# Top-256 search of a sparse attention: the largest score tiles counted by sums of signs on ScalarE instead of by comparisons on VectorE, with one more pass for equal scores

## The chip, the cores and the metric

The kernel runs on one core of a Trainium2 chip. The metric is the device time of one execution in microseconds (us). The profile shows the engines of that core: PE is TensorE's matrix multiply (PEld its weight loads), DVE is VectorE, ACT is ScalarE, POOL is GpSimd, SP is SyncE. In this program SP issues the transfers.

## The reference, cut to what matters

The program is a decoder trunk of two layers over 1024 tokens of width 1024. Each layer has an input projection, three groups of attention heads, an output projection, a gated FFN and a gated embedding. One of the groups is sparse: every query keeps only the 256 earlier positions with the highest index score, and its softmax runs over those.

```python
ilog = jnp.einsum('bqhd,bkd->bqhk', sl(idx_q), idx_k) * IDX_DIM ** -0.5
isc = jnp.einsum('bqhk,bqh->bqk', jax.nn.relu(ilog), sl(idx_w)).astype(jnp.float32)
isc = jnp.where(causal[None], isc, -jnp.inf)
_, sel = lax.top_k(isc, topk)          # topk = 256; of equal scores the earlier positions
valid = sel <= qpos[None, :, None]
...
a = jnp.where(valid[:, None], a, -jnp.inf)
pa = jax.nn.softmax(a, axis=-1).astype(vg.dtype)
```

## The kernel before

The tokens are handled in two halves of 512. For each layer and half there is dense work (`in_projection`, `layer_rest`: `gemm` with three matmuls for each 128x128 block of weights, lines 266 to 268) and attention work (`attention`). `weave` (line 64) interleaves the two by weights, so that the attention of one part runs between the dense matmuls of another. PE's order is written out by the program itself; for the other engines a scheduler decides the order from priorities. Every engine works through its own order strictly from front to back.

`attention(L, half)` begins with `indexer`, which fills the score tile `isc` (lines 1046 to 1050). It holds one block of columns for each query tile of 128 tokens that can have more than 256 candidates: in half 0 tiles of 384 and 512 columns, in half 1 of 640, 768, 896 and 1024. Then a list of steps is worked off, five stick-breaking heads, six latent heads, five sparse heads. A step of a head has its parts in `scores` (line 788, into PSUM), `piece` (line 828, PE transposes the probabilities into PSUM tile T), `post_piece` (lines 835 and 836: ACT rounds T to the high part of `PT`, DVE subtracts to get the low part) and `pv` (line 845, PE multiplies `PT` with the values into O).

The search, `topk` (lines 1070 to 1114), is a generator that runs in the background of the stick and latent heads. It finds the 256th largest score of each row bit by bit: 31 times (line 1094) `count` compares each tile with that row's candidate and adds up the hits (line 1082, one DVE instruction for each tile, followed in the trace by a read of its accumulator), line 1096 turns the counts into a bit, line 1097 sets the next candidate. A first count decides the sign of the threshold, a last one counts the scores above it, and lines 1107 to 1113 turn `isc` into a mask. All of this is on DVE. The loop that works off the steps gives the search a credit with each step (`TOPK_W`, lines 57, 1156 and 1172) and draws pieces of it while credit is left (line 1176); before the first sparse head it draws the rest (line 1167):

```python
background = topk()
tk = TOPK_W[half] / max(first_sparse - 1, 1)
...
credit += tk * (TOPK_RATE[0] if step < SB_H * nb else TOPK_RATE[1])
...
    while credit > 0:
        credit -= next(background, 1e9)
```

Other lines that the prediction names: `rstd` (lines 344 to 352), twelve small DVE instructions in a chain that give the norm of 512 tokens, with `replicate` (line 360) on PE behind them; line 187, ACT's rounding of a weight tile; `norm` of a pair of heads (line 938), which copies sums into the small tile `wide` for PE to transpose; line 888, DVE's scan of a stick head; line 874, ACT's exponential with its sum.

Of the kernel before, what the change touches and what calls it, by code (L numbers as in the profile page):

```python
# [8 lines left out]
F32 = mybir.dt.float32  # L9
R = mybir.dt.float32r  # L10
BF = mybir.dt.bfloat16
I32 = mybir.dt.int32
AF = mybir.ActivationFunctionType
ALU = mybir.AluOpType
AX = mybir.AxisListType

T = 1024
# [4 lines left out]
HALF = 512  # L22
# [4 lines left out]
TOPK = 256  # L27
EPS = 1e-6
NEG = -1e30
# [12 lines left out]
PTS, AS, VS = 2, 2, 2  # L42
# [11 lines left out]
LAG = (3, 3)  # L54
DENSE = {"in": 1188, "full": 2622, "last": 2028}
ATT = (256, 500, 356, 400)
TOPK_W = (51, 157)


def f32(ap):  # L60
# [28 lines left out]
def trunk(ctx: ExitStack, tc, x, p, w_in, attn_norm, mla_q_norm, mla_w_uq, mla_kv_norm, mla_w_ukv,  # L89
# [3 lines left out]
    PE, ACT, DVE, POOL = nc.tensor, nc.scalar, nc.vector, nc.gpsimd  # L93
# [7 lines left out]
    ap = pool("ap", 1)  # L101
    sm = pool("sm", 4)
# [613 lines left out]
    def attention(L, half):  # L716
        k = (L, half)
        nk = HALF * (half + 1)
        tiles = [4 * half + i for i in range(4)]
        itiles = [t for t in tiles if t >= 2]  # L720
        off, o = {}, 0
        for t in itiles:
            off[t] = o
            o += 128 * (t + 1)
        isc = ap.tile([128, 3328], F32, name="isc")

        def have(*keys):
            return all(clock[0] - stored.get(key, 1e9) >= DELAY for key in keys)
# [175 lines left out]
        class Head:  # L904
# [26 lines left out]
            def norm(self):  # L931

                j = self.i // 2
                if self.done and j in rows:
                    self.n = n = 64 if self.i % 2 == 0 else 128
                    self.S = S_tile()[:, 0]
                    wide = sm.tile([128, 4, 2, 64], F32, name="wide", bufs=1)
                    ACT.copy(wide[:, :, :n // 64], rows[j].rearrange("p h t -> p t h")[:, :, :n // 64].unsqueeze(
                        3).to_broadcast([128, 4, n // 64, 64]))
                    for t in range(4):  # L940
                        PE.transpose(self.S[:n, t * 128:(t + 1) * 128],
                                     wide[:, t, :n // 64].rearrange("p h c -> p (h c)"), identF)
# [126 lines left out]
                    yield 0.5 + (t + 1) * 0.5  # L1069
        def topk():  # L1070

            ni = len(itiles)

            def small(name, dt):
                return sm.tile([128, 4], dt, name=name, bufs=1)[:, :ni]
            cnt, xm, cand, inc = small("cnt", F32), small("xm", I32), small("cand", I32), small("inc", I32)
            junk = ap.tile([128, T], mybir.dt.uint8, name="junk")

            def count(c, op):
                for i, t in enumerate(itiles):  # L1080
                    n = 128 * (t + 1)
                    DVE.tensor_scalar(junk[:, :n], isc[:, off[t]:off[t] + n], c[:, i:i + 1], None,  # L1082
                                      op0=op, op1=ALU.add, accum_out=cnt[:, i:i + 1])
                    yield 0.13 + n / 960

            DVE.memset(cand, 0)
            yield from count(cand.bitcast(F32), ALU.is_ge)


            DVE.tensor_scalar(inc, cnt, float(TOPK), None, op0=ALU.is_ge)  # L1090
# [1 line left out]
            DVE.tensor_scalar(xm, inc, -1, None, op0=ALU.bitwise_xor)  # L1092
            DVE.tensor_scalar(cand, xm, 1 << 30, None, op0=ALU.bitwise_xor)
            for b in range(30, -1, -1):
                yield from count(cand.bitcast(F32), ALU.is_ge)
                DVE.tensor_scalar(inc, cnt, float(TOPK), float(1 << b), op0=ALU.is_lt, op1=ALU.mult)
                DVE.scalar_tensor_tensor(cand, inc, (1 << b) >> 1, cand, op0=ALU.bitwise_xor, op1=ALU.bitwise_xor)
                yield 0.2
            thr = cand.bitcast(F32)
            yield from count(thr, ALU.is_gt)  # L1100
            DVE.tensor_scalar(cnt, cnt, -1.0, float(TOPK), op0=ALU.mult, op1=ALU.add)
            for i, t in enumerate(itiles):
                n = 128 * (t + 1)
                s = isc[:, off[t]:off[t] + n]
                c = slice(i, i + 1)
# [3 lines left out]
                                       op0=ALU.mult, op1=ALU.add)  # L1109
# [45 lines left out]
        background = topk()  # L1155
        tk = TOPK_W[half] / max(first_sparse - 1, 1)
        credit = 0.0
# [141 lines left out]
```

## Time and profile before

| | |
|---|---|
| median of 3 runs | 3207.02 us (3206.75 to 3208.24) |
| the profiled execution's own time | 3211.26 us |
| its span, first to last instruction | 3209.1 us |
| PE busy | 3068.6 us (96%) |
| DVE busy | 2099.0 us (65%) |
| ACT busy | 1486.3 us (46%) |
| POOL busy | 1722.9 us (54%) |
| DVE's counts for the search (line 1082 with the reads of its accumulator) | 371.3 + 32.1 us |

Busy times of a whole span are averages over stages with different limits. The stages matter here: the profile cuts the span into 40 slices of 80 us and gives each engine's busy tenths, and the trace can be asked for any stretch. The search runs in four stretches, one for each layer and half, of which the two of half 1 are the long ones.

### The profile page before, as it was taken

To read this page: it belongs to the slowest core of one execution; us is meant where nothing else is said; L and a number is where in the kernel's file an instruction comes from. 1 tells how busy PE (TensorE), PEld (TensorE's weight loads), DVE (VectorE), ACT (ScalarE), POOL (GpSimd) and SP (SyncE) were. 2 spreads that over 40 slices of the span, in tenths; PEclk is the share of its full clock that TensorE was granted. 3 is DMA by queue.
4 is the path that set the end of the run, shared out by engine and by line. 5 is a ranking of instruction groups with operands and counts; after the bars stand their busy time and mean duration, and the time that the engine had idled before them with its cause. 6 is when DMAs were issued, how large, how long until landed. Compare 5 with 4: busy or idle time off the path is not lost. (4 is left out here: it accounts for less than half of the span.)

```text
span 3209.1 us, 43576 instructions
## 1 busy us (share of the span) xinstructions
PE 3068.6 (96%) x15059; PEld 2549.1 (79%) x15059; DVE 2099.0 (65%) x3701; ACT 1486.3 (46%) x2485; POOL 1722.9 (54%) x1980
## 2 busy tenths in 40 slices
PE   8889999999998999999999999889999999999998
PEld 7768888777887888888888788767888877888877
DVE  4878656799997646687744636899997465322234
ACT  4555654445445545444444535544444455322234
POOL 4533356666445433765555744656445445766665
PEclk9999999999999999999999999999999999999999
DMA  7465453323233346433333465422333323333322
GB/s 203 117 194 147 144 172 96 91 89 96 90 97 93 105 116 176 132 103 107 107 104 89 116 162 176 116 72 86 98 97 95 89 70 113 117 99 94 98 92 73
DMA packets 549949, 363.59 MB, mean 113 GB/s; under 512 B 134672, under 2 KB 491744, under 8 KB 549728
## 3 DMA queue, kind: packets, MB, share of 16 engines
q1 hardware_dynamic: 549727, 360.81, 38.7%
q8 instruction: 119, 1.95, 0.3%
q14 instruction: 103, 0.84, 0.1%
HBM read 310.65 MB, written 50.08 MB: 112 GB/s over the span
## 5 line engine op out<-in xcount | busy, mean ns | idle before, releaser
L196 POOL TENSOR_TENSOR wl<-wr,wh 128x256 fp32r<-128x256 f32 x1684 | 1375.4, 848 | 1178.5 <-ACT wh L187 1143.9
L266 PE MATMUL D<-act,wh 128*128 128x512 f32 x3416 | 1363.6, 399 | 31.6 <-DVE h L582 16.5
L267 PE MATMUL D<-act,wh 128*128 128x512 f32 x3416 | 1341.0, 393 | 2.3 <-DVE act L633 2.0
L268 PE MATMUL D<-act,wl 128*128 128x512 f32 x3416 | 1340.0, 392 | 2.4 <-POOL wl L196 2.4
L266 PEld LDWEIGHTS D<-act,wh 128*128 128x128 f32 x3416 | 646.0, 189 | 174.7 <-issue 14.1
L268 PEld LDWEIGHTS D<-act,wl 128*128 128x128 f32 x3416 | 645.3, 189 | 145.9 <-POOL wl L196 4.8
L187 ACT CAST wh<-wr 128x1024 fp32r<-128x1024 f32 (+3 forms) x432 | 443.6, 1027 | 665.6 <-PE D L267 525.5
L267 PEld LDWEIGHTS D<-act,wh 128*128 128x128 f32 x3416 | 646.6, 189 | 126.6 <-DVE act L633 3.1
L1082 DVE TENSOR_SCALAR_CACHE_REDUCE junk<-isc,cand 128x512 uint8<-128x512 f32 (+5 forms) x396 | 371.3, 938 | 5.5
L836 DVE TENSOR_TENSOR PT<-T,PT 128x384 fp32r<-128x384 f32 (+1 forms) x320 | 201.8, 631 | 139.9 <-ACT PT L835 138.9
L835 ACT CAST PT<-T 128x384 fp32r<-128x384 f32 (+1 forms) x320 | 173.6, 542 | 192.4 <-PE T L828 181.4
L845 PEld LDWEIGHTS O<-PT,V 128*128 128x128 f32 x1280 | 196.2, 190 | 72.2 <-DVE PT L836 43.7
L845 PE MATMUL O<-PT,V 128*128 128x256 f32 x1280 | 215.5, 287 | 38.1 <-DVE PT L836 34.3
L891 POOL TENSOR_TENSOR P<-P,A 128x127 f32<-128x127 f32 (+3 forms) x80 | 101.0, 1266 | 198.3 <-DVE A L888 122.1
L788 PE MATMUL S<-kh,qh 128*128 128x384 f32 (+4 forms) x544 | 206.6, 381 | 0.3 <-ACT P L1042 0.3
L788 PE MATMUL S<-kl,qh 128*128 128x384 f32 (+4 forms) x544 | 203.8, 375 | 1.6 <-DVE kl L293 1.6
L828 PE MATMUL T<-identF,P 128*128 128x128 f32 x1152 | 182.2, 277 | 17.5 <-POOL P L891 6.6
L828 PEld LDWEIGHTS T<-identF,P 128*128 128x128 f32 x1152 | 135.4, 142 | 21.9 <-POOL P L891 9.0
L1048 DVE SCALAR_TENSOR_TENSOR isc<-P,iw,isc 128x384 f32<-128x384 f32 (+2 forms) x84 | 97.0, 1157 | 78.4 <-ACT P L1042 78.3
L619 POOL TENSOR_TENSOR tmp<-tmp,rr 128x512 f32<-128x512 f32 x88 | 120.2, 1366 | 32.4 <-DVE tmp L618 27.0
L630 DVE SCALAR_TENSOR_TENSOR tmp<-tmp,D 128x512 f32<-128x512 f32 x88 | 60.1, 683 | 107.6 <-POOL tmp L619 80.3
L853 ACT COPY o<-O 64x256 f32<-64x256 f32 x128 | 47.3, 370 | 175.4 <-PE O L845 174.0
(217 smaller groups left out, 3304.4 us busy)
## 6 DMA issues: line engine op xcount, KB each, us to landing
wr<-in_w_gate_dram SPq DMA_DIRECT2D x88, 512.0 KB, 3.8
wr<-in_w_up_dram SPq DMA_DIRECT2D x88, 512.0 KB, 3.8
wr<-in_w_down_dram SPq DMA_DIRECT2D x80, 512.0 KB, 3.4
wr<-in_w_in_dram SPq DMA_DIRECT2D x44, 512.0 KB, 3.8
wr<-in_w_in_dram SPq DMA_DIRECT2D x76, 256.0 KB, 3.8
wr<-in_w_o_dram SPq DMA_DIRECT2D x32, 512.0 KB, 4.3
wr<-in_w_ple_gate_dram SPq DMA_DIRECT2D x32, 512.0 KB, 3.8
h<-h SPq DMA_DIRECT2D x56, 256.0 KB, 4.4
```

The lines of the kernel that those rows point to most:

```text
L187: ACT.copy(hi, raw)
L196: POOL.tensor_tensor(l[:, ks], a[:, ks], f32(h[:, ks]), op=ALU.subtract)
L266: PE.matmul(ps, a, ah, start=first and i == 0, stop=False)
L267: PE.matmul(ps, a, al, start=False, stop=False)
L268: PE.matmul(ps, b, ah, start=False, stop=last and i == len(ks) - 1)
L619: POOL.tensor_tensor(t, t, ffn.rep, op=ALU.mult)
L788: PE.matmul(o, a, b, start=j == 0, stop=j == len(mms) - 1)
L828: PE.transpose(ps[:, o:o + 128], self.P[q][:, j * 128:(j + 1) * 128], identF)
L835: ACT.copy(pt[:, 0, o:], self.ps[:, o:])
L836: DVE.tensor_sub(pt[:, 1, o:], self.ps[:, o:], f32(pt[:, 0, o:]))
L845: PE.matmul(self.O[:, :256], self.head.V[:, j, :], pt[:, s, o:o + 256], start=j == 0 and s == 0, stop=j == 2 * self.n - 1 and s == 1)
L1082: DVE.tensor_scalar(junk[:, :n], isc[:, off[t]:off[t] + n], c[:, i:i + 1], None, op0=op, op1=ALU.add, accum_out=cnt[:, i:i + 1])
```

## The change

In each half the last tiles (one of 512 columns in half 0; those of 896 and 1024 in half 1, the first padded with -1e30 to 1024) are no longer compared by DVE in the 31 rounds. ACT takes sign(2^24 * (candidate - score)) over the tile and sums it, which is the number of scores below the candidate less the number above it. A small ACT instruction scales the candidates first (`bias`), and one more DVE instruction of each round turns the sums into bits. Since a score equal to the candidate adds 0 to a sum of signs, the rounds can end one step off where scores are equal; after them one more count of all tiles against the next larger number, with nine small DVE instructions, settles that. `wide` no longer has a tile of its own and takes a buffer of the tile name `A` (2 buffers, also used by the stick heads' line 886 and by the search's lines 1106 to 1113). The credits follow the shorter DVE work.

```diff
-TOPK_W = (51, 157)
+TOPK_W = (40, 96)
+SCALE, LEAST = 2.0 ** 24, 2.0 ** -126
...
+        na, wa = ((1, 512), (2, 1024))[half]
         off, o = {}, 0
-        for t in itiles:
+        for i, t in enumerate(itiles):
             off[t] = o
-            o += 128 * (t + 1)
-        isc = ap.tile([128, 3328], F32, name="isc")
+            o += 128 * (t + 1) if i < len(itiles) - na else wa
+        isc = ap.tile([128, 3456], F32, name="isc")
+        for t in itiles[-na:]:
+            if 128 * (t + 1) < wa:
+                POOL.memset(isc[:, off[t] + 128 * (t + 1):off[t] + wa], NEG)
...
-                    wide = sm.tile([128, 4, 2, 64], F32, name="wide", bufs=1)
+                    wide = ap.tile([128, T], F32, name="A", bufs=AS)[:, :HALF].rearrange(
+                        "p (t h c) -> p t h c", t=4, h=2)
...
+            nv = ni - na
...
+            def signs(i):
+                o = off[itiles[nv + i]]
+                ACT.activation(junk2[:, :wa], isc[:, o:o + wa], AF.Sign, scale=-SCALE, bias=bias[:, i:i + 1],
+                               accum_out=sgn[:, i:i + 1])
...
             for b in range(30, -1, -1):
-                yield from count(cand.bitcast(F32), ALU.is_ge)
-                DVE.tensor_scalar(inc, cnt, float(TOPK), float(1 << b), op0=ALU.is_lt, op1=ALU.mult)
+                ACT.activation(bias, c[:, nv:], AF.Copy, scale=SCALE)
+                for i in range(max(nv, na)):
+                    if i < na:
+                        signs(i)
+                    if i < nv:
+                        yield count(i, c, ALU.is_ge)
+                DVE.tensor_scalar(inc[:, :nv], cnt[:, :nv], float(TOPK), float(1 << b), op0=ALU.is_lt, op1=ALU.mult)
+                DVE.tensor_scalar(inc[:, nv:], sgn, float(wa + 1 - 2 * TOPK), float(1 << b), op0=ALU.is_gt, op1=ALU.mult)
                 DVE.scalar_tensor_tensor(cand, inc, (1 << b) >> 1, cand, op0=ALU.bitwise_xor, op1=ALU.bitwise_xor)
-                yield 0.2
-            thr = cand.bitcast(F32)
-            yield from count(thr, ALU.is_gt)
+                yield 0.4
+
+            nxt, ok = small("nxt", F32), small("ok", F32)
+            DVE.tensor_scalar(nxt.bitcast(I32), cand, 0x7fffffff, None, op0=ALU.bitwise_and)
+            DVE.tensor_scalar(ok, nxt, LEAST, None, op0=ALU.is_ge)
+            DVE.tensor_mul(c, c, ok)
+            DVE.tensor_scalar(nxt, nxt, 0.6 * 2.0 ** -23, None, op0=ALU.mult)
+            DVE.tensor_add(nxt, nxt, c)
+            for i in range(ni):
+                yield count(i, nxt, ALU.is_ge)
+            DVE.tensor_scalar(ok, cnt, float(TOPK), None, op0=ALU.is_ge)
+            DVE.tensor_sub(nxt, nxt, c)
+            DVE.tensor_mul(nxt, nxt, ok)
+            DVE.tensor_add(c, c, nxt)
+            thr = c
+            for i in range(ni):
+                yield count(i, thr, ALU.is_gt)
```

PE's order is the same before and after, but for the name of the tile that line 938's sums are transposed from. The orders of DVE and ACT move. In the changed program's listing the lines stand higher: 344 to 352 become 345 to 353, 835 and 836 become 841 and 842, 888 becomes 894, 1082 becomes 1095; 1114 is the small `bias`, 1101 the sum of signs, 1120 and 1121 the two bit instructions.

The first place is DVE in layer 1, half 1, where the first norm that falls into the search computes its `rstd` (the FFN norm of layer 1's half 0). Before, its first twelve instructions from `ms` on are these; the chain goes on to a third `rstd` with four more counts between (640, 768, 896, 1024 columns):

```order
2303 L344 TENSOR_SCALAR ms<-T 128x4
2304 L1082 TENSOR_SCALAR junk,cnt<-isc,cand 128x768
2305 L347 TENSOR_SCALAR rtmp<-ms 128x4
2306 L1082 TENSOR_SCALAR junk,cnt<-isc,cand 128x896
2307 L348 TENSOR_SCALAR rstd<-rtmp 128x4
2308 L1082 TENSOR_SCALAR junk,cnt<-isc,cand 128x1024
2309 L350 TENSOR_TENSOR rtmp<-rstd 128x4
2310 L836 TENSOR_TENSOR PT<-T,PT 128x512
2311 L1096 TENSOR_SCALAR inc<-cnt 128x4
2312 L351 SCALAR_TENSOR_TENSOR rtmp<-rtmp,ms 128x4
2313 L888 SCALAR_TENSOR_TENSOR A<-A,zeros 128x768
2314 L1097 SCALAR_TENSOR_TENSOR cand<-inc,cand 128x4
```

The same chain in the changed program, on DVE from `ms` to one row before the last `rstd`, which follows directly behind the last row shown:

```order
2308 L1095 TENSOR_SCALAR junk,cnt<-isc,cand 128x768
2309 L348 TENSOR_SCALAR rtmp<-ms 128x4
2310 L349 TENSOR_SCALAR rstd<-rtmp 128x4
2311 L351 TENSOR_TENSOR rtmp<-rstd 128x4
2312 L352 SCALAR_TENSOR_TENSOR rtmp<-rtmp,ms 128x4
2313 L353 SCALAR_TENSOR_TENSOR rstd<-rtmp,rstd 128x4
2314 L351 TENSOR_TENSOR rtmp<-rstd 128x4
2315 L352 SCALAR_TENSOR_TENSOR rtmp<-rtmp,ms 128x4
2316 L353 SCALAR_TENSOR_TENSOR rstd<-rtmp,rstd 128x4
2317 L351 TENSOR_TENSOR rtmp<-rstd 128x4
2318 L352 SCALAR_TENSOR_TENSOR rtmp<-rtmp,ms 128x4
2319 L842 TENSOR_TENSOR PT<-T,PT 128x512
```

Seven counts, a scan and two small instructions of the search stood inside the chain; now one count does, and the one `PT` subtraction that was there before.

The second place is ACT in layer 0, half 1, in the middle of the search, around the roundings of T into `PT`. Before:

```order
534 L835 CAST PT<-T 128x512
535 L886 ACTIVATE A<-S 128x896
536 L887 ACTIVATE P<-S 128x896
537 L187 CAST wh<-wr 128x1024
538 L835 CAST PT<-T 128x512
539 L834 CAST PT<-zeros 128x2x128
```

And the same heads in the changed program:

```order
613 L841 CAST PT<-T 128x512
614 L892 ACTIVATE A<-S 128x896
615 L893 ACTIVATE P<-S 128x896
616 L188 CAST wh<-wr 128x1024
617 L1114 ACTIVATE bias<-cand 128x2
618 L1101 ACTIVATE junk_6380,sgn<-isc,bias 128x1024 x2
619 L841 CAST PT<-T 128x512
620 L840 CAST PT<-zeros 128x2x128
```

Between two roundings ACT now has `bias`, which waits for DVE's `cand`, and two sums of signs. In the 31 rounds of the two half-1 stretches there are 95 such roundings: 11 have two sums directly ahead of them as here, 25 have one, 59 have none. In half 0 it is 3 of 38, each with one.

## Rows read from the trace of the kernel before

**Rows 1.** The page: busy time of engines, and tenths of 40 slices.

```profile
PE 3068.6 (96%) x15059; PEld 2549.1 (79%) x15059; DVE 2099.0 (65%) x3701; ACT 1486.3 (46%) x2485; POOL 1722.9 (54%) x1980
...
DVE  4878656799997646687744636899997465322234
```

**Rows 2.** Windows: engines' busy us, clock; four search stretches, then three others.

```profile
core 0: us, PE busy (x) PEld busy (x) DVE busy (x) ACT busy (x) POOL busy (x), PEclk, DMA share, GB/s
105.00:305.00 200.00, 179.36 (x927) 146.07 (x928) 170.24 (x418) 108.73 (x237) 84.23 (x109) 0.97 0.54 148
610.00:980.00 370.00, 344.47 (x1760) 286.43 (x1759) 359.15 (x581) 175.36 (x273) 195.16 (x209) 0.99 0.30 89
1350.00:1590.00 240.00, 235.47 (x1163) 196.05 (x1162) 187.42 (x395) 114.80 (x220) 151.93 (x177) 1.00 0.36 107
2035.00:2410.00 375.00, 341.85 (x1719) 284.03 (x1717) 357.23 (x591) 178.25 (x275) 197.27 (x209) 0.96 0.30 89
400.00:600.00 200.00, 196.67 (x914) 163.40 (x913) 114.63 (x144) 91.27 (x128) 121.83 (x133) 1.00 0.43 125
980.00:1280.00 300.00, 289.71 (x1525) 244.43 (x1524) 173.71 (x329) 154.38 (x270) 126.36 (x153) 0.99 0.46 125
320.00:400.00 80.00, 77.79 (x442) 67.61 (x441) 52.28 (x133) 52.12 (x119) 28.65 (x34) 1.00 0.47 141
```

**Rows 3.** Waits of PE, 2035 to 2410: us in total, times, longest.

```profile
PE O L845 <- DVE PT L836: 16.6, 12, 3.9
PE T L360 <- DVE rstd L352: 8.2, 1, 8.2
```

**Rows 4.** Timeline, 2086 to 2103: start, us, engine, line, operation [idle before].

```profile
2086.89 0.16 DVE L344 TENSOR_SCALAR ms<-T 128x4 f32<-128x4 f32 x1
...
2099.34 1.09 PE L360 MATMUL T<-identF,rstd 128*128 128x128 f32 x4 [8.20 <-DVE rstd L352]
...
2101.08 0.63 PE L268 MATMUL D<-act,wl 128*128 128x512 f32 x1
2101.51 0.63 PE L266 MATMUL D<-act,wh 128*128 128x512 f32 x1
```

**Rows 5.** DVE by line and shape, the search: count, busy us, mean ns.

```profile
L1082 DVE TENSOR_SCALAR_CACHE_REDUCE junk<-isc,cand 128x1024 uint8<-128x1024 f32 x66 | 83.7, 1268 | 0.3
L1082 DVE TENSOR_SCALAR_CACHE_REDUCE junk<-isc,cand 128x896 uint8<-128x896 f32 x66 | 74.9, 1135 | 0.5
L1082 DVE TENSOR_SCALAR_CACHE_REDUCE junk<-isc,cand 128x768 uint8<-128x768 f32 x66 | 66.1, 1001 | 0.5
L1082 DVE TENSOR_SCALAR_CACHE_REDUCE junk<-isc,cand 128x640 uint8<-128x640 f32 x66 | 57.8, 875 | 1.7
L1082 DVE TENSOR_SCALAR_CACHE_REDUCE junk<-isc,cand 128x512 uint8<-128x512 f32 x66 | 48.7, 737 | 0.9
L1082 DVE DVE_READ_ACCUMULATOR junk<-isc,cand 128x1 f32 x396 | 32.1, 81 | 0.0
L1096 DVE TENSOR_SCALAR inc<-cnt 128x2 int32<-128x2 f32 x62 | 19.0, 307 | 0.7
```

**Rows 6.** ACT by line and shape: exponentials with a sum.

```profile
L874 ACT ACTIVATE P<-P,nm 128x1024 f32<-128x1024 f32 x10 | 11.5, 1151 | 14.1 <-DVE nm L872 14.1
L874 ACT ACTIVATE P<-P,nm 128x512 f32<-128x512 f32 x10 | 7.2, 723 | 10.3 <-DVE nm L872 10.3
L874 ACT ACTIVATION_READ_ACCUMULATOR P<-P,nm 128x1 f32 x60 | 11.2, 186 | 0.0
```

**Rows 7.** Timeline, 710 to 716: one `PT` from transposes to its use.

```profile
710.37 0.60 PE L828 MATMUL T<-identF,P 128*128 128x128 f32 x4
711.06 0.59 ACT L835 CAST PT<-T 128x512 fp32r<-128x512 f32 x1
713.12 0.68 DVE L836 TENSOR_TENSOR PT<-T,PT 128x512 fp32r<-128x512 f32 x1
715.95 0.28 PE L845 MATMUL O<-PT,V 128*128 128x256 f32 x1
```

More of the change, by code (lines that the diff above doesn't have):

```diff
@@ L1076, in topk, with count @@
             cnt, xm, cand, inc = small("cnt", F32), small("xm", I32), small("cand", I32), small("inc", I32)
+            sgn, bias = small("sgn", F32)[:, :na], small("bias", F32)[:, :na]
+            c = cand.bitcast(F32)
             junk = ap.tile([128, T], mybir.dt.uint8, name="junk")
[L1079 to L1084, printed above, removed]
+            junk2 = ap.tile([128, T], mybir.dt.uint8, name="junk2")
+            def count(i, c, op):
+                t = itiles[i]
+                n = 128 * (t + 1)
+                DVE.tensor_scalar(junk[:, :n], isc[:, off[t]:off[t] + n], c[:, i:i + 1], None,
+                                  op0=op, op1=ALU.add, accum_out=cnt[:, i:i + 1])
+                return 0.13 + n / 960
+            def signs(i):
+                o = off[itiles[nv + i]]
+                ACT.activation(junk2[:, :wa], isc[:, o:o + wa], AF.Sign, scale=-SCALE, bias=bias[:, i:i + 1],
+                               accum_out=sgn[:, i:i + 1])
             DVE.memset(cand, 0)
-            yield from count(cand.bitcast(F32), ALU.is_ge)
+            for i in range(ni):
+                yield count(i, c, ALU.is_ge)
             DVE.tensor_scalar(inc, cnt, float(TOPK), None, op0=ALU.is_ge)
@@ L1094, in topk @@
             for b in range(30, -1, -1):
-                yield from count(cand.bitcast(F32), ALU.is_ge)
-                DVE.tensor_scalar(inc, cnt, float(TOPK), float(1 << b), op0=ALU.is_lt, op1=ALU.mult)
-                DVE.scalar_tensor_tensor(cand, inc, (1 << b) >> 1, cand, op0=ALU.bitwise_xor, op1=ALU.bitwise_xor)
-                yield 0.2
-            thr = cand.bitcast(F32)
-            yield from count(thr, ALU.is_gt)
+                ACT.activation(bias, c[:, nv:], AF.Copy, scale=SCALE)
[3 more added lines that the diff above has]
+                    if i < nv:
+                        yield count(i, c, ALU.is_ge)
+                DVE.tensor_scalar(inc[:, :nv], cnt[:, :nv], float(TOPK), float(1 << b), op0=ALU.is_lt, op1=ALU.mult)
+                DVE.tensor_scalar(inc[:, nv:], sgn, float(wa + 1 - 2 * TOPK), float(1 << b), op0=ALU.is_gt, op1=ALU.mult)
+                DVE.scalar_tensor_tensor(cand, inc, (1 << b) >> 1, cand, op0=ALU.bitwise_xor, op1=ALU.bitwise_xor)
+                yield 0.4
[12 more added lines that the diff above has]
+            thr = c
+            for i in range(ni):
+                yield count(i, thr, ALU.is_gt)
             DVE.tensor_scalar(cnt, cnt, -1.0, float(TOPK), op0=ALU.mult, op1=ALU.add)
```

## The prediction

> **What bounds the kernel now.** I read the busy times first [rows 1]: PE is busy 96% of the span, DVE 65%, ACT 46%. By these shares PE is the bound and DVE has room. The slices in the same group say where that is untrue: DVE stands at 9 tenths in two blocks of slices, and these are the two half-1 searches. The windows [rows 2] give the four search stretches one by one. In 610 to 980 DVE is busy 359.15 of 370 us (97%) and PE idles 370 - 344.47 = 25.5 us; in 2035 to 2410 DVE is busy 95% and PE idles 33.2 us. Together that is 58.7 us of idle PE in 745 us, or 7.9%. The half-0 searches are milder: 20.6 us of idle PE at 85% DVE in 105 to 305, 4.5 us (1.9%) at 78% DVE in 1350 to 1590. Where attention runs without a search, PE idles 1.7% (400 to 600) and 3.4% (980 to 1280), with DVE at 57 and 58%. So PE is the bound of the kernel, and in the half-1 searches a full DVE takes some 5 points of PE's time. In such a stretch ACT is busy only 47%.
>
> What the waits look like is in the stretch from 2035 [rows 3]: 16.6 us in 12 waits of the value product for a `PT` that DVE subtracts late, and one wait of 8.2 us for `rstd`. The timeline [rows 4] opens that one: DVE begins `ms` at 2086.89, PE gets the last `rstd` at 2099.34. The chain's small instructions take about 0.16 us each; the 12.4 us are seven counts, a scan, a subtraction and the small search instructions standing between them. After it PE's granted clock is at the lower level, 1.2 of 2.4 GHz: its matmuls follow each other by 0.43 us (2101.08, 2101.51).
>
> **What the change takes from DVE.** In each half-1 search 31 rounds lose the tiles of 1024 and 896 columns with two accumulator reads: 31 x (1.268 + 1.135 + 2 x 0.081) = 79.5 us [rows 5]. Each round gains a bit instruction, 31 x 0.307 = 9.5 us. The extra pass costs one count of each tile, 1.268 + 1.135 + 1.001 + 0.875 + 4 x 0.081 = 4.6 us, and nine small instructions, 9 x 0.307 = 2.8 us. Net 62.6 us: DVE goes from 359 to about 297 of 370 us (80%), in the later stretch from 357 to 295 of 375 (79%). In half 0 the same sum is 31 x 0.818 - 9.5 - 1.6 - 2.8 = 11.5 us. Over the program DVE loses some 148 of its 2099 us, nearly all of it where it is full.
>
> **What it adds to ACT.** No row shows a sum of signs. The nearest is the exponential from SBUF with a sum of its own: 1.151 us for 1024 columns, 0.723 for 512, and 0.186 for the accumulator read [rows 6]. `bias` works on two numbers for each row; I price it like that read, 0.19 us. A half-1 round is then 2 x 1.337 + 0.19 = 2.86 us, 31 rounds 88.8 us; a half-0 search 31 x 1.10 = 34.1 us. ACT rises from 175 to 264 of 370 us (71%) in half 1. The order shows as many loads of ACT's function tables after as before, so none is priced.
>
> A count on either engine costs the same here: 1.268 + 0.081 = 1.349 us on DVE, 1.151 + 0.186 = 1.337 us on ACT for 1024 columns [rows 5, 6]. The Trainium skill, ScalarE: Activation LUTs, Rules for kernel authors, speaks against such a move: elementwise work belongs on VectorE, which it puts at up to about three times the speed, in bf16. With f32 scores the trace does not bear that out; if DVE could count at three times the speed, the move would save it a third as much, about 26 us less the same additions.
>
> **What that is worth on the path.** The span ends when PE's own order ends, so the gain is idle PE that goes away. For the half-1 stretches the good end is the idle share beside a half-full DVE, 1.7%: 745 x 0.017 = 13 us are left and 46 us are gained. I take 3.4% (as in 980 to 1280), since ACT will stand at 71%, and the fullest ACT in the rows (65% in 320 to 400) goes with 2.8% idle PE. That leaves 25 us and **gains 33 us**. Some 8 of these are the `rstd` wait: in the changed order the chain holds one count and one subtraction, so from 2086.89 it takes 12 x 0.16 + 1.08 + 0.68 = 3.7 us, and PE, which ran dry at 2091.1, finds it finished. With 0.31 us for each small instruction it would be late by 1.2 us.
>
> The clock: the granted 0.96 in 2035 to 2410 lacks 15 us of full speed, the 0.99 in 610 to 980 another 4, the 0.97 in the first stretch 6 [rows 2]. Much of that falls on idle time and is already counted. Behind the `rstd` wait seven matmuls, of which the rows show two, took 0.2 us more each than the usual 0.23, 1.4 us in all [rows 4]. With about a dozen long waits I take **5 us**, between 0 and 12 (half of the sum).
>
> The half-0 searches: DVE falls from 85 to 79% in the first, but ACT rises from 54 to 71%. I take 0, between a gain of 10 (half of the 20.6 us idle) and a loss of 3 (signs ahead of 3 of 38 roundings, 1.1 us each).
>
> Small edits at zero: the padding is one POOL memset in each layer, and POOL is half idle there. `wide` in a buffer of `A` shares with stick heads that are done by then and with the search's last steps; a copy can wait there for the mask steps of a tile, which I bound by three counts of 1024 columns, 4 us. The pace of the search stays, since `TOPK_W` was lowered with its work; the mask steps stand at nearly the same steps as before.
>
> **Against it** stands what now lies in front of ACT's rounding of `PT`. One such path took from 710.97 (transposes done) to 715.95 (product), 5.0 us, of which rounding and subtraction used 1.27 and DVE's lateness 1.5 [rows 7]. So about 2.2 us were spare, 3.7 with a free DVE. Of 95 roundings in the half-1 rounds 25 have one sum ahead (1.34 us) and 11 have two (2.67 us). Fully exposed that is 33.5 + 29.4 = 63 us, the bad end. A free DVE gives the path 1.5 us back, more than one sum takes; so I take none of it beyond the 3.4%.
>
> Sum: 33 + 5 + 0 = 38 us. The profiled span 3209.1 becomes 3171, that execution with the 2.2 us around its span 3173; the median of the runs lay 4.2 us below the profiled execution, so the median comes to **3169 us**.
>
> **The rivals.**
> 1. *Full relief.* ACT's half-empty queue absorbs the sums, idle PE falls to 1.7%, half of the lost clock returns and half of the first stretch's idle goes: 46 + 12 + 10 = 68 us, 3139 us. For it: the `rstd` chain in the new order. Against it: ACT is then the fuller engine of the `PT` path.
> 2. *No gain.* PE is at 96%, and its idle time in the search is the interleaving's own, so that a wait for DVE turns into one for ACT a moment later: 3207 us, give or take 5. For it: PE waits for many lines, not for the counts themselves; even without a search it idles up to 3.4%. Against it: DVE at 97% has nothing it could wait for. The Trainium skill, Perfetto Trace Analysis, Identifying the Most-Contended Engine, has one improve the engine with the highest occupancy; by the whole span that is PE, and this change gives PE nothing. The trace disagrees in the two stretches of [rows 2], where DVE is the fuller one.
> 3. *Slower: the sums block the rounding.* DVE's bit instruction waits for ACT's sums, ACT's `bias` waits for DVE's candidate, and both queues are strictly in order. If each engine carries the other's lateness, the 63 us of sums ahead of roundings are all exposed, against 38 gained: 25 us slower, 3232 us. It decides where the spare 2.2 to 3.7 us are used up, that is once over 60% of the 63 us (38) reach PE. For it: ACT's roundings, which today wait for PE alone, now wait for DVE too.
>
> **How the numbers follow.** A measurement of this kernel tells about 0.2% (6 us) from no change. Chances: the forecast 0.50 (3150 to 3190), full relief 0.18, no gain 0.13, slower 0.19. The first two are faster by over 0.2%, so faster has 0.68, same 0.13 and slower 0.19. The range starts below full relief at 3135, takes in the no-gain case, and ends at 3214, which leaves out most of the slower case.
>
> **What would show it.** Right: in the two half-1 stretches DVE near 80% and ACT near 71%, idle PE near 25 us in place of 58.7, the `rstd` wait gone, a granted clock of 0.98 or more from 2035 on, a sum of signs near 1.15 us. Wrong: waits of PE for `PT` as long as before with ACT's rounding behind a sum, or DVE idle in front of the bit instruction on `sgn`; then rival 3 or 2 holds. Signs much dearer than 1.15 us would undo the price of ACT, and a wait at the copy into `A` the zero for `wide`.

## The result: slower by half a per cent

| | before | changed |
|---|---|---|
| median of 4 runs each | 3207.63 us (3206.75 to 3213.64) | 3225.98 us (3223.98 to 3229.74) |
| ratio, 95% interval | | 1.0052 [1.0040, 1.0064] |
| span of the profiled execution | 3209.1 us | 3222.2 us |
| PE busy; span less PE busy | 3068.6; 140.5 us | 3082.0; 140.2 us |
| mean granted clock | 0.987 | 0.982 |

The prediction was 3169 us with a range from 3135 to 3214. It was wrong, and on the other side: slower, where faster had the larger chance. The time is near the 3232 us of the third rival. The profiled executions are not the median ones: that of the kernel before lies above its median (3211.26 us), that of the changed kernel is the fastest of its four (3223.98), so the spans are 13.1 us apart where the ratio gives 17.

The page after the change, with the two lines that answer to [rows 1], the busy times and DVE's tenths:

```profile
PE 3082.0 (96%) x15059; PEld 2561.0 (79%) x15059; DVE 1963.2 (61%) x3513; ACT 1690.1 (52%) x2981; POOL 1740.7 (54%) x1982
...
DVE  4866656787787636676644546788786465322234
```

DVE lost 135.8 us, and the blocks of nines are gone. PE has the same number of instructions and as much idle time as before; what grew is its busy time, by 13.4 us, and the span grew by 13.1. A granted clock of 0.987 over 3209.1 us lacks 42 us of full speed, 0.982 over 3222.2 us lacks 58. Each clock is rounded to 0.001, 3.2 us of the span. Within that, the two profiles put the whole difference between them into matmuls that ran at the lower of the two levels.

The windows of the changed kernel, with the columns and the four search stretches of [rows 2]:

```profile
core 0: us, PE busy (x) PEld busy (x) DVE busy (x) ACT busy (x) POOL busy (x), PEclk, DMA share, GB/s
105.00:305.00 200.00, 179.11 (x929) 145.21 (x928) 153.12 (x399) 137.54 (x333) 87.54 (x108) 0.98 0.54 147
610.00:980.00 370.00, 342.48 (x1705) 283.68 (x1704) 304.33 (x499) 245.22 (x419) 198.05 (x206) 0.96 0.29 87
1350.00:1590.00 240.00, 236.85 (x1168) 196.79 (x1167) 169.01 (x387) 143.85 (x313) 156.88 (x177) 1.00 0.35 106
2035.00:2410.00 375.00, 341.87 (x1680) 283.77 (x1679) 308.91 (x510) 251.38 (x425) 203.83 (x212) 0.95 0.29 86
```

In the half-1 stretches DVE fell from 97 and 95% to 82% in both, and ACT rose from 47 and 48% to 66 and 67%. Idle PE is 27.5 and 33.1 us, before 25.5 and 33.2. Relief came to DVE, and none of it to PE.

Cut by stage, these stretches show more. The steps of the stick-breaking heads run in 610 to 830 and 2045 to 2290, those of the latent heads behind them. The same columns, first the kernel before:

```profile
610.00:830.00 220.00, 200.16 (x1009) 165.67 (x1008) 214.89 (x341) 107.85 (x161) 133.04 (x134) 0.98 0.28 85
830.00:990.00 160.00, 152.72 (x792) 127.06 (x791) 153.43 (x253) 73.23 (x124) 65.61 (x80) 1.00 0.30 93
2045.00:2290.00 245.00, 214.52 (x1060) 177.38 (x1059) 232.72 (x376) 117.88 (x178) 135.89 (x137) 0.94 0.27 80
2290.00:2430.00 140.00, 133.95 (x690) 111.97 (x689) 133.97 (x222) 62.36 (x105) 61.74 (x73) 0.99 0.31 92
```

Then the changed kernel:

```profile
610.00:830.00 220.00, 192.87 (x926) 157.96 (x925) 184.46 (x285) 151.59 (x255) 128.02 (x125) 0.93 0.27 81
830.00:990.00 160.00, 157.81 (x825) 132.49 (x824) 126.01 (x221) 96.83 (x171) 73.63 (x84) 1.00 0.31 94
2045.00:2290.00 245.00, 214.75 (x1029) 176.81 (x1028) 206.21 (x324) 172.15 (x289) 141.99 (x139) 0.92 0.27 80
2290.00:2430.00 140.00, 137.69 (x713) 116.18 (x712) 113.02 (x201) 83.90 (x146) 62.13 (x74) 0.99 0.34 101
```

Under the latent heads the change does what was forecast: idle PE falls from 7.3 to 2.2 us and from 6.0 to 2.3. Under the stick heads it does the opposite. In 610 to 830 PE idles 27.1 in place of 19.8 us, its clock falls from 0.98 to 0.93, and it gets through 926 matmul instructions in place of 1009; in 2045 to 2290 it gets through 1029 in place of 1060.

A window holds somewhat different work in the two kernels, but PE's order is the same in both, so the time between two given matmuls can be compared. From the matmul that the kernel before starts at 610 us to the one at 830 the changed kernel takes 15.8 us longer, from 2045 to 2290 4.6 us longer; in the stretches of the latent heads, to 990 and to 2430, it is 3.9 and 5.1 us shorter. A stretch without a search differs by up to 5 us between these two profiles, so the clear loss is the one under the stick heads of layer 0.

Where a stick head's time goes is in the timeline of the changed kernel, 738 to 748, of which a few rows stand here (start, duration, engine, line, operation, and in brackets idle time before it):

```profile
737.12 2.53 POOL L620 TENSOR_TENSOR tmp<-tmp,rr 128x512 f32<-128x512 f32 x1
...
738.48 1.19 DVE L1120 TENSOR_SCALAR inc<-cnt 128x2 int32<-128x2 f32 x1
...
739.61 1.32 POOL L897 TENSOR_TENSOR P<-P,A 128x639 f32<-128x639 f32 x1
...
739.77 1.17 DVE L1122 SCALAR_TENSOR_TENSOR cand<-inc,cand 128x4 int32<-128x4 int32 x1
...
740.40 0.60 PE L834 MATMUL T<-identF,P 128*128 128x128 f32 x4
...
741.04 0.20 ACT L1114 ACTIVATE bias<-cand 128x2 f32<-128x2 f32 x1 [3.70 <-DVE cand L1122]
...
741.27 1.15 ACT L1101 ACTIVATE junk<-isc,bias 128x1024 uint8<-128x1024 f32 x1
...
742.33 0.19 ACT L1101 ACTIVATION_READ_ACCUMULATOR junk<-isc,bias 128x1 f32 x1
742.42 1.03 ACT L188 CAST wh<-wr 128x1024 fp32r<-128x1024 f32 x1
...
743.36 1.15 ACT L1101 ACTIVATE junk<-isc,bias 128x1024 uint8<-128x1024 f32 x1
...
744.50 0.60 ACT L633 CAST act<-tmp 128x512 fp32r<-128x512 f32 x1
745.01 0.57 ACT L841 CAST PT<-T 128x512 fp32r<-128x512 f32 x1
...
746.13 0.68 DVE L842 TENSOR_TENSOR PT<-T,PT 128x512 fp32r<-128x512 f32 x1
...
746.87 0.62 PE L851 MATMUL O<-PT,V 128*128 128x256 f32 x3 [0.52 <-DVE PT L842]
```

This answers to [rows 7]. The transposes are done at 741.00, and ACT's rounding (line 841) begins at 745.01, 4.0 us later. Two sums, a weight rounding and an FFN rounding stand ahead of it. But before all that ACT stood still for 3.70 us, because `bias` waited for DVE's `cand`, with the weight rounding behind it in the queue. Of the whole delay PE here lost only 0.52 us, in front of the value product; other `PT` cost it more, as the waits under relief show below. The Trainium skill, PSUM — Partial Sum Buffer, Engine vs sequencer instructions, calls the queues of ScalarE and VectorE strict FIFO; these rows agree, with those 3.70 us. Over the whole program ACT's wait in front of `bias`, which did not exist before, is the first of these two rows of the waits (us in total, times, longest):

```profile
ACT bias L1114 <- DVE cand L1122: 132.5, 80, 5.8
...
DVE inc L1121 <- ACT junk L1101: 3.9, 11, 0.6
```

### The profile page after: what moved, and what is told of

It is laid out like the page before. It is cut to its first block, busy times and chain, and to the rows that moved or that the text cites. A ratio compares the mean times of both kernels' runs of the same rounds, so it can differ in the third digit from the quotient of the medians.

```text
span 3222.2 us, 43878 instructions
## 1 busy us (share of the span) xinstructions
PE 3082.0 (96%) x15059; PEld 2561.0 (79%) x15059; DVE 1963.2 (61%) x3513; ACT 1690.1 (52%) x2981; POOL 1740.7 (54%) x1982
## 5 line engine op out<-in xcount | busy, mean ns | idle before, releaser
L197 POOL TENSOR_TENSOR wl<-wr,wh 128x256 fp32r<-128x256 f32 x1684 | 1391.1, 857 | 1196.6 <-ACT wh L188 1157.9
L267 PE MATMUL D<-act,wh 128*128 128x512 f32 x3416 | 1367.4, 400 | 33.1 <-DVE h L583 14.8
L851 PE MATMUL O<-PT,V 128*128 128x256 f32 x1280 | 215.0, 288 | 45.6 <-DVE PT L842 36.6
L1101 ACT ACTIVATE junk<-isc,bias 128x1024 uint8<-128x1024 f32 (+1 forms) x186 | 187.4, 1008 | 3.8
L1095 DVE TENSOR_SCALAR_CACHE_REDUCE junk<-isc,cand 128x384 uint8<-128x384 f32 (+4 forms) x210 | 176.3, 839 | 3.7
L1055 DVE SCALAR_TENSOR_TENSOR isc<-P,iw,isc 128x384 f32<-128x384 f32 (+2 forms) x84 | 97.2, 1159 | 78.9 <-ACT P L1049 78.7
L583 DVE TENSOR_TENSOR h<-h,D 128x512 f32<-128x512 f32 x144 | 97.6, 681 | 58.7 <-PE D L269 58.3
```

The lines of the kernel that those rows point to most:

```text
L197: POOL.tensor_tensor(l[:, ks], a[:, ks], f32(h[:, ks]), op=ALU.subtract)
L267: PE.matmul(ps, a, ah, start=first and i == 0, stop=False)
L851: PE.matmul(self.O[:, :256], self.head.V[:, j, :], pt[:, s, o:o + 256], start=j == 0 and s == 0, stop=j == 2 * self.n - 1 and s == 1)
L1101: ACT.activation(junk2[:, :wa], isc[:, o:o + wa], AF.Sign, scale=-SCALE, bias=bias[:, i:i + 1], accum_out=sgn[:, i:i + 1])
```

## The experiments

All ratios are to the kernel before, run on the same chip; 0.1% is 3.2 us. A difference between two of the runs below has an interval of some 0.2% (6 us) to either side. relief, load, wait, load_paced and wait_paced leave out part of the exchange between ACT and DVE and so select other scores; the other runs compute the complete result. Line numbers are those of the changed kernel, where an edit has not moved them by a few.

### What each part costs alone

**relief**: DVE's relief without the work on ACT.

```diff
-                ACT.activation(bias, c[:, nv:], AF.Copy, scale=SCALE)
...
-                    if i < na:
-                        signs(i)
...
-                DVE.tensor_scalar(inc[:, nv:], sgn, float(wa + 1 - 2 * TOPK), float(1 << b), op0=ALU.is_gt, op1=ALU.mult)
+                DVE.tensor_scalar(inc[:, nv:], sgn, -1.0 if b == 30 else 1.0, float(1 << b), op0=ALU.is_gt, op1=ALU.mult)
...
+            DVE.memset(sgn, 0)
```

> Leaves out ACT's part of the search altogether (no bias, no sums of signs; the bit instruction on the sums reads a constant), so the selection is another one; DVE's part is that of the change. Theory A (cross wait: DVE's relief is worth about what was forecast, and ACT's bias at the head of ACT's queue, waiting for DVE's candidate, eats it): 3155 to 3185 us. Theory B (load: the sums' own time on ACT eats it): the same 3155 to 3185. Theory C (a full DVE was never the cause of PE's idle time): 3200 to 3210.

Measured: 3178.03 us, ratio 0.9902 [0.9887, 0.9916]. This is the gain that DVE's relief can give, some 31 us, with the extra pass in it. The windows under the stick heads:

```profile
610.00:830.00 220.00, 206.03 (x1041) 171.84 (x1041) 198.61 (x317) 110.97 (x165) 136.93 (x137) 0.98 0.30 88
...
2045.00:2290.00 245.00, 225.93 (x1139) 188.57 (x1139) 214.61 (x358) 120.18 (x182) 134.73 (x141) 0.96 0.29 87
```

With DVE at the same work as in the changed kernel but ACT as before, PE idles 14.0 and 19.1 us there, and the clock is back at 0.98 and 0.96. So the full DVE was a true limit, and what the change lost it lost by what it put on ACT: 1.0052 less 0.9902 is 1.5%, 48 us.

Where PE pays for it is in the waits of the value product for `PT`, first for DVE's part, then for ACT's rounding. The kernel before, relief, and the changed kernel:

```profile
PE O L845 <- DVE PT L836: 34.3, 26, 3.9
PE O L845 <- ACT PT L835: 0.9, 1, 0.9
...
PE O L851 <- DVE PT L842: 24.1, 14, 5.4
PE O L851 <- ACT PT L841: 0.8, 1, 0.8
...
PE O L851 <- DVE PT L842: 36.6, 19, 6.2
PE O L851 <- ACT PT L841: 7.0, 6, 2.9
```

Relief's span is 45.6 us shorter than that of the changed kernel. Of these, 25.1 are idle PE (115.1 against 140.2 us), and 18.7 of the 25.1 are the two waits above; the other 20.5 are PE's busy time, the same matmuls at a lower granted clock.

**load**: the sums run on ACT, but with a constant bias, and nobody reads them; the bit instruction is that of relief.

```diff
-                               accum_out=sgn[:, i:i + 1])
+                               accum_out=sgn2[:, i:i + 1])
...
-                ACT.activation(bias, c[:, nv:], AF.Copy, scale=SCALE)
...
+            DVE.memset(sgn, 0)
+            DVE.memset(bias, 0)
```

> As relief, but ACT does its sums of signs with a constant bias into a tile that nobody reads: ACT's load without a wait in either direction in the rounds. Theory A: within 8 us of relief. Theory B: near the change, 3215 to 3230. Theory C: 3215 to 3230, what the load adds to the kernel before.

Measured: 3212.53 us, ratio 1.0003 [0.9991, 1.0014]. That lies between the ranges of the theories, nearer to B. Work on ACT that waits for nothing already eats the relief, where it stands ahead of the step's own. But without a wait to space them the sums bunch: in ACT's order the 62 of a half-1 search stand within some 180 rows, in the changed kernel within some 285. So this run overstates what the work alone costs, and `load_paced` below was made for that.

**wait**: as load, but `bias` is taken from DVE's candidate again; only DVE's reading of the sums is missing.

```diff
-                               accum_out=sgn[:, i:i + 1])
+                               accum_out=sgn2[:, i:i + 1])
...
+            DVE.memset(sgn, 0)
```

> As load, but each round's bias is computed from DVE's candidate as in the change (ACT waits for DVE); DVE still reads no sum. Theory A: near the change, 3215 to 3230, with ACT's bias waiting 100 us or more in all. Theory B: within 6 us of load, wherever load is.

Measured: 3228.80 us, ratio 1.0049 [1.0032, 1.0066], with 133.4 us of `bias` waiting for `cand` in 77 waits. That is the changed kernel's time within the interval. DVE's wait for ACT's sums, half of what the third rival blamed, costs nothing that can be measured; ACT's wait for DVE is what is there.

**pass**: the extra pass and `wide` in a buffer of `A`, with all counts on DVE.

```diff
-TOPK_W = (40, 96)
+TOPK_W = (52, 161)
...
+                for i in range(ni):
+                    yield count(i, c, ALU.is_ge)
+                DVE.tensor_scalar(inc, cnt, float(TOPK), float(1 << b), op0=ALU.is_lt, op1=ALU.mult)
```

> The extra pass and the shared tile of the sums alone: all counts stay on DVE, no work on ACT. Theory A and the forecast (the pass is some 7 us of DVE in a half-1 search that is full anyway, the shared tile costs nothing): 3208 to 3222 us, at most 10 above the kernel before. A rival, that the shared tile A makes ACT wait for the mask steps: 3225 or more.

Measured: 3219.85 us, ratio 1.0027 [1.0016, 1.0039]. The small edits cost some 9 us where DVE is still full. In this run the copy into `A` waits 2.7 us in 4 waits for the search's mask steps, and PE never waits for the copy, so it can hold little of the 9 us.

### Where ACT's part stands in ACT's order

**queue**: the complete change, but what the search issues in a step goes behind the step's other ACT work in the scheduler's order.

```diff
-            with tc.issue_after(last):
+            lact = next((i for i in reversed(nc.cur_bb.bb.instructions) if i.engine == ACT.engine), None)
+            with tc.issue_after(last), tc.issue_after(lact):
```

> The change, complete, with one edit: what the search issues on ACT stands behind ACT's other work of the step, as the search's DVE work already does. Theory A: the bias waits fall to less than half of 132.5 us, roundings have fewer sums ahead of them, 3170 to 3200 us. Theory B: the load is the same, 3215 to 3230.

Measured: 3208.32 us, ratio 0.9989 [0.9979, 0.9998]. Two lines win back 0.63%, 20 us. The wait of `bias` falls from 132.5 to 97.2 us. Theory A had the direction, but neither the wait (under half) nor the time (to 3200) came as low as it said.

**load_paced**: load with the edit of queue.

```diff
-                ACT.activation(bias, c[:, nv:], AF.Copy, scale=SCALE)
...
-            with tc.issue_after(last):
+            with tc.issue_after(last), tc.issue_after(lact):
```

> As load (sums of signs with a constant bias, read by nobody, selection another one), but issued on ACT behind the step's other ACT work, so that they are spread as in the run queue instead of bunched early. If the bunching made load dear: 3185 to 3200 us. If the sums' own time on ACT is what costs: 3205 to 3215, as load. Against queue (3208) the difference is the waits between the two engines.

Measured: 3187.43 us, ratio 0.9927 [0.9912, 0.9942]. Where the sums stand behind the step's work and wait for nothing, they cost 0.25% beside relief, 8 us (1 to 15 by the intervals), and not the 1.0% of load.

**wait_paced**: wait with the edit of queue.

```diff
-            with tc.issue_after(last):
+            with tc.issue_after(last), tc.issue_after(lact):
```

> As the run wait (sums of signs on ACT with a bias taken from DVE's candidate, sums read by nobody, bit instruction on a constant, so another set of scores is selected and the output is not the reference's), but ACT's part of the search is issued behind the step's other ACT work, as in the run queue. It splits the 0.62% between load_paced (ratio 0.9927, no wait across the engines) and queue (0.9989, both waits). Theory A (ACT's wait for the candidate holds up the rest of ACT's queue; DVE's wait for the sums costs next to nothing, as between wait and the changed kernel): 0.998, that is about as slow as queue, with ACT's bias waiting 90 us or more for cand. Theory B (DVE's wait for the sums is what costs once the sums stand late in ACT's order): 0.993 to 0.994, about as fast as load_paced. In between, the two share it.

Measured: 3214.16 us, ratio 1.0002 [0.9993, 1.0012]. It is as slow as queue, or slower. Between load_paced and wait_paced stands ACT's wait for the candidate, with the small `bias` instructions: 0.75%, 24 us. DVE's wait for the sums again adds nothing. So load_paced, load, wait_paced and wait make a square: the wait for the candidate costs 24 us with the sums behind the step's work and 15 with them ahead of it, and the place ahead costs 24 us without the wait, with the bunching of load in it, and 15 with it.

**skewq**: queue, with `bias` and the sums of half 1 issued one count later in the round. Here the candidate is older when ACT comes to it. The complete computation again.

```diff
+                if nv > 1:
+                    yield count(0, c, ALU.is_ge)
                 ACT.activation(bias, c[:, nv:], AF.Copy, scale=SCALE)
-                for i in range(max(nv, na)):
-                    if i < na:
-                        signs(i)
-                    if i < nv:
-                        yield count(i, c, ALU.is_ge)
+                for i in range(na):
+                    signs(i)
+                yield count(nv - 1, c, ALU.is_ge)
```

> The complete computation of the run queue, but in half 1 ACT's bias and the two sums of a round are issued one count later (behind the round's first count on DVE, beside its second), so that DVE's candidate is older when ACT comes to it, and the sums are younger when DVE's bit instruction reads them. The half-0 searches, with one count on DVE in a round, stay as in queue. Theory A (what costs is ACT standing still in front of bias; DVE's wait for the sums costs next to nothing): the wait of bias for cand falls from 97 us to 60 or less, DVE's wait of inc for the sums rises from 7 us, and the time comes some way toward load_paced, ratio 0.994 to 0.997. Theory B (the loss follows the round trip between the engines, whichever of them waits): the wait only changes its place, ratio 0.998 to 1.000, or more where DVE now waits.

Measured: 3192.73 us, ratio 0.9943 [0.9930, 0.9955]. The waits on ACT and DVE, in the form shown above:

```profile
ACT bias L1116 <- DVE cand L1122: 55.1, 39, 4.1
...
DVE inc L1121 <- ACT junk L1101: 13.6, 24, 2.6
```

and its windows under the stick heads:

```profile
610.00:830.00 220.00, 204.50 (x1031) 169.88 (x1031) 196.53 (x314) 167.51 (x283) 132.58 (x137) 0.98 0.30 89
...
2045.00:2290.00 245.00, 219.94 (x1119) 182.06 (x1118) 215.65 (x358) 184.37 (x317) 142.97 (x141) 0.98 0.29 86
```

ACT is busier in these windows than in the changed kernel (167.5 against 151.6 us, since the work gets on faster), yet PE gets through 1031 matmul instructions in place of 926 and the clock is 0.98 in place of 0.93. The load of ACT as such was not the trouble. ACT's wait fell by 42 us from queue and DVE's rose by 7, and the time fell by 0.46%, 15 us: the wait did not just change its place. The number of sums directly ahead of a rounding, by which the prediction priced the danger, does not explain it: between the first and the last sum of the half-1 searches that is 35 of 92 roundings in the changed kernel, 28 in queue and 31 in skewq.

### Using ACT only where it has room

**late120**: in half 1 the rounds that fall under stick heads count all tiles on DVE, those under latent heads leave two to ACT; a faster credit.

```diff
-TOPK_W = (40, 96)
+TOPK_W = (40, 120)
...
+                if stick[0]:
+                    for i in range(ni):
+                        yield count(i, c, ALU.is_ge)
+                    DVE.tensor_scalar(inc, cnt, float(TOPK), float(1 << b), op0=ALU.is_lt, op1=ALU.mult)
+                else:
...
+            stick[0] = half == 1 and step < SB_H * nb
```

> The change, complete, but in half 1 the rounds drawn during the five stick-breaking heads count all four tiles on DVE, and only the rounds during the latent heads use ACT (credits 120 for the mixed work). Theory D (the sums cost where ACT also has the two sigmoids of each stick tile, and gain where it has not): 3190 to 3205 us, below the kernel before. Theory B (the load costs wherever it lies): 3210 to 3225.

Measured: 3196.33 us, ratio 0.9954 [0.9938, 0.9971], in the range of theory D. The window of this run under the stick heads of layer 0:

```profile
610.00:830.00 220.00, 209.48 (x1062) 174.79 (x1061) 200.46 (x309) 123.10 (x188) 139.04 (x139) 0.98 0.31 93
```

The change's loss under the stick heads is gone, but it is not the change's gain under the latent heads that is kept. Along PE's order, as above, this run is 10.6 and 15.5 us shorter than the kernel before under the stick heads, where relief gains 6.5 and 10.5; under the latent heads it is 3.5 us longer and 3.4 shorter. Under the stick heads the search is also drawn more slowly, for all its larger credit, since a round there counts four tiles: 12 rounds stand in DVE's order ahead of the last scan of a stick head, 19 in the change and 16 before. So two things differ there, the sums on ACT and the pace of the search, and no run sets them apart.

**late120q**: late120 with the two lines of queue.

```diff
-            with tc.issue_after(last):
+            with tc.issue_after(last), tc.issue_after(lact):
```

> late120 with the search's ACT work behind the step's other ACT work, as in queue. Theories A and D together: 3185 to 3202 us, the fastest complete one. If D holds alone, the same as late120 within 5 us.

Measured: 3192.42 us, ratio 0.9939 [0.9924, 0.9954]. That is in the range of theories A and D together, but 3.9 us from late120 and within its interval, so it does not tell them from D alone.

**late140q**: the same with more credit, so that more rounds fall under the stick heads.

```diff
-TOPK_W = (40, 120)
+TOPK_W = (40, 140)
```

> The complete computation of late120q (in half 1 the rounds that fall under stick heads count all four tiles on DVE, those under latent heads leave two tiles to ACT; ACT's part behind the step's other ACT work) with the search drawn faster in half 1 (credit 140 in place of 120): more rounds fall under the stick heads, fewer need ACT. Theory A (ACT's share is what costs): no slower than late120q, ratio 0.992 to 0.994. Theory B (a full DVE under the stick heads is what costs): the faster pace presses more counts into the stick heads, DVE over 95% there, and part of the gain is lost, ratio 0.996 or more.

Measured: 3202.68 us, ratio 0.9968 [0.9957, 0.9980]. Slower than late120q: with 14 rounds in place of 12 ahead of the last scan of a stick head half of the gain goes. This is theory B's ratio. DVE is busy 207.07 of 220 us in 610 to 830 (94%), in late120q 204.62 (93%), so that DVE's limit is back fits, but rests on a small step in its share.

**late_skewq**: late120q with the edit of skewq.

```diff
                 else:
+                    if nv > 1:
+                        yield count(0, c, ALU.is_ge)
                     ACT.activation(bias, c[:, nv:], AF.Copy, scale=SCALE)
...
+                    for i in range(na):
+                        signs(i)
+                    yield count(nv - 1, c, ALU.is_ge)
```

> late120q with the same edit as in skewq: in the rounds of half 1 that fall under latent heads, ACT's bias and sums are issued one count later. Complete computation. Theory A: a little faster than late120q (0.9939), 0.992 to 0.994, since few rounds are left on ACT in half 1 and its bias waits only 40 us there in all. Theory B: unchanged or slower, 0.994 to 0.996.

Measured: 3196.35 us, ratio 0.9955 [0.9939, 0.9970]. It is not faster than late120q, as the first theory had it, and not slower by more than the intervals allow. `bias` waits 28.9 us in place of 39.7, too little to see.

So late120q and skewq beat both kernels by some 18 to 20 us against before and 1.1% against the change. Their intervals overlap, and relief, which no complete version reached, shows another 0.4% above them.

## Why the prediction was wrong, step by step

- **What bounds the kernel**: right. A full DVE held up PE in the half-1 searches; taking its counts away is worth 31 us (relief), where 38 were forecast (33 and 5 for the clock). The interval of relief reaches to 36. Its profile has 25.4 us less idle PE and 7.1 us less busy PE than the kernel before.
- **What it takes from DVE**: 135.8 us measured, 148 forecast. DVE stands at 82%, not 79 to 80. Of the 12 us, 9.4 are line 1122, the next candidate, whose mean for four columns rose from 452 to 603 ns, 62 times.
- **What it adds to ACT**: the prices held. These rows of the changed kernel, by line and form, answer to [rows 5, 6]:

```profile
L1101 ACT ACTIVATE junk<-isc,bias 128x1024 uint8<-128x1024 f32 x124 | 142.6, 1150 | 2.2
L1101 ACT ACTIVATE junk<-isc,bias 128x512 uint8<-128x512 f32 x62 | 44.8, 723 | 1.6
L1101 ACT ACTIVATION_READ_ACCUMULATOR junk<-isc,bias 128x1 f32 x186 | 35.2, 189 | 0.0
L1114 ACT ACTIVATE bias<-cand 128x2 f32<-128x2 f32 x62 | 12.6, 202 | 99.0 <-DVE cand L1122 95.6 <-DVE cand L1112 3.4
...
L1122 DVE SCALAR_TENSOR_TENSOR cand<-inc,cand 128x4 int32<-128x4 int32 x62 | 37.4, 603 | 1.4
L1121 DVE TENSOR_SCALAR inc<-sgn 128x2 int32<-128x2 f32 x62 | 18.9, 305 | 1.0 <-ACT junk L1101 1.0
```

  A sum of signs takes 1.150 us where 1.151 were taken, its read 0.189 for 0.186, `bias` 0.202 for 0.19. ACT rose by 203.8 us in all and stands at 66 to 67%, not 71, mainly since the read of an accumulator begins before its sum has ended (in the timeline above at 742.33, and the next instruction starts 1.15 us after the sum did). What the sum did not contain stands at the end of the row on `bias`: 99.0 us of idle ACT ahead of 62 instructions.
- **The step that failed** is under "Against it": "so I take none of it beyond the 3.4%". The price of what stands ahead of ACT's roundings was taken as zero, from a bad end of 63 us. Measured, it is 48 us (the changed kernel against relief), 76% of the bad end, and past the 60% from which the third rival was to decide. The step also priced the wrong thing. It counted sums that stand directly ahead of a rounding. The runs show two other terms: ACT's wait for DVE's candidate, worth 15 us between load and wait and 24 between load_paced and wait_paced; and the place of the search's work ahead of the step's own, worth 24 us between load and load_paced and 20 between the change and queue. The two overlap: from relief to the run wait, 8 us for the sums themselves, 24 for their place and 15 for the wait make 47 of the 48 us. And the spare time was read from one path [rows 7].
- **The `rstd` wait**: it went from 8.2 to 1.8 us, where 0 to 1.2 were forecast. But the stretch kept its long wait, on another line. The waits of PE in 2035 to 2410, in answer to [rows 3]:

```profile
PE O L851 <- DVE PT L842: 21.5, 9, 6.2
...
PE T L361 <- DVE rstd L353: 1.8, 1, 1.8
```

  The 6.2 us stand close by, 77 matmul instructions earlier in PE's order. The timeline of the changed kernel, 2079 to 2089, in answer to [rows 4]:

```profile
2079.11 0.49 PE L834 MATMUL T<-identF,P 128*128 128x128 f32 x3
...
2080.30 1.17 ACT L1101 ACTIVATE junk<-isc,bias 128x1024 uint8<-128x1024 f32 x1
2080.35 2.28 DVE L894 TENSOR_TENSOR_SCAN A<-A,zeros 128x1024 f32<-128x1024 f32 x1
...
2081.43 0.50 ACT L841 CAST PT<-T 128x384 fp32r<-128x384 f32 x1
...
2087.06 1.00 DVE L1095 TENSOR_SCALAR_CACHE_REDUCE junk<-isc,cand 128x768 uint8<-128x768 f32 x1
...
2087.99 0.55 DVE L842 TENSOR_TENSOR PT<-T,PT 128x384 fp32r<-128x384 f32 x1
...
2088.59 1.01 PE L851 MATMUL O<-PT,V 128*128 128x256 f32 x3 [6.23 <-DVE PT L842]
```

  ACT rounds 1.8 us after the transposes, with a sum directly ahead; then DVE goes through a scan, two counts, a split and two instructions of the dense part before its subtraction at 2087.99. In the windows 2080 to 2100 the granted clock is 0.74, before it was 0.82. That one stall would give way to another close by was not priced.
- **The clock**: forecast as a gain of 5 us. Relief alone has a gain of 7 (0.989 over 3176.6 us lacks 35), the change a loss of 16 (the 58 less 42 us above). Under the stick heads the trace's clock records show the lower level 8 times before, 38 us in all, and 12 times in the changed kernel, 68 us; each time PE stood in a wait or had just left one, of 1.8 to 8.2 us before and of 2.0 to 6.2 after. That more waits of such length brought the clock down is argued from these two traces; no run set it apart, and the longest wait alone does not decide: queue has one of 7.2 us for `PT` at a mean clock of 0.986, pass none for `PT` over 3.9 us at 0.982.
- **The zeros**: the half-0 searches came out at zero, with 20.9 and 3.2 us of idle PE for 20.6 and 4.5. `wide` in `A` makes ACT wait 2.7 us at line 945 for the mask steps, and PE once 2.6 us for that copy, within the bound of 4. The pace did not stay: 19 rounds stand in DVE's order ahead of the last scan of a stick head where 16 stood, which puts more sums under the stick heads; no run shows what that alone costs. The extra pass was in the sum as DVE time only; with the other small edits it measures 9 us on the path (pass).
- **The rivals**: the third named the wait that counts, ACT's for the candidate, with a chance of 0.19. Its other wait, DVE's for the sums, is 3.9 us in all. That its time came near is partly luck: it set 63 us against 38 gained, where 48 against 31 were measured, and the 63 priced sums ahead of roundings, which by themselves cost 8. The second rival's picture, a wait for DVE that turns into one for ACT, shows too: the value product's wait for ACT's rounding rose from 0.9 to 7.0 us.

## What to carry to other kernels

When work moves from a full engine to a half-empty one and its result is needed back, price the round trip: each instruction that waits for the other engine stops everything queued behind it, and an average share of 47% does not show what is queued there. Put the receiving engine's part behind its urgent work and issue it some steps after its operand, so that the operand is old; here two lines and one shifted count turned a loss of 0.5% into a gain of 0.6%. Measure the relief alone first, by leaving the moved work out: it gives the most that the move can bring at the same pace of the moved work.

## What had not been expected of the hardware

A small DVE instruction can last as long as a POOL instruction beside it. In the timeline above line 1122, with four columns, runs from 739.77 to 740.94, and POOL's line 897, which began at 739.61, ends at 740.93. Alone it takes as little as 0.145 us; its mean for four columns is 0.603. Of these 62 in the changed kernel, 30 took over 0.5 us, and all 30 ended 0.02 us behind a POOL instruction that had started before them. The Trainium skill, SBUF — State Buffer, Who interferes with whom, says that a DVE instruction with two inputs in SBUF contends with a GpSimd instruction that reads SBUF. Line 1122 reads `inc` and `cand`, and its two ends 0.01 us apart agree. But two inputs are not needed here: line 1120, which reads `cnt` alone, runs from 738.48 to 739.67 in that timeline, and POOL's line 620 ends at 739.65; 16 more of its 62 with two columns last over 0.4 us and end so. Here this candidate is what ACT's `bias` waits for, so POOL's length became part of ACT's wait.

PE's idle time as a whole said nothing about the change: 140.5 us before and 140.2 after, with 13 us between the spans. One has to look at the granted clock beside it. Against relief, with 115.1 us, it shows about half of the loss.
